# A priority above the mixers' early jobs for every weight piece of a hybrid decoder layer

## The chip, the cores and the metric

The kernel runs on one core of one Trainium2 chip. The metric is the device time of one execution in microseconds (us). Where three runs are shown, the median stands with the lowest and the highest. The profile is that of one execution, taken by the hardware profiler; its engines are PE (TensorE matmuls, with PEld for the weight loads into the array), DVE (VectorE), ACT (ScalarE), POOL (GpSimd) and SP, whose queue (SPq) issues most of the DMAs.

## The reference

One layer on 1024 tokens of width 1024, batch 1, all in float32:

```python
x = x + 0.5 * swiglu(rms_norm(x, ffn1_norm), w_gate1, w_up1, w_down1)   # 1024 -> 2816 -> 1024
x = x + hybrid_mixer(rms_norm(x, mix_norm), w_in, ..., w_out)
x = x + 0.5 * swiglu(rms_norm(x, ffn2_norm), w_gate2, w_up2, w_down2)
return rms_norm(x, final_norm)
```

The mixer projects the normed input once (`w_in`) and gives half of the columns to an HGRN2 recurrence (4 heads of 128, evaluated in chunks of 64 tokens) and half to an RWKV-7 recurrence (8 heads of 64, whose state is updated token by token in the reference). The outputs of both go through `w_out`.

## The kernel before

**Tiling.** Activations are kept with the features on the 128 partitions and 512 tokens along the free axis, so the sequence is two blocks, b=0 and b=1. A weight matrix is read in pieces of 128 x 512 float32 (256 KB). Each product is done as three matmuls in a rounded float32 format: a value is split into a rounded part `hi` and the remainder `lo`, and hi x hi, hi x lo and lo x hi are summed (`mm3`, lines 99 to 101).

**A piece of weights.** `load_piece` makes one: a DMA on SP's queue into `w_raw` (L76), the rounding to `w_hi` on ACT and the subtraction that gives `w_lo` on DVE (`split`, L67 and L68). `w_raw` has 7 buffers in the first and the last stage and 5 in the middle one; `w_hi` and `w_lo` have 3 each, for the whole program. A piece of four 128 x 128 weight tiles feeds 12 matmuls. The units of the feed-forward stages, which combine gate and up for both blocks with fewer products, load and split their pieces by functions of their own (`unit`, `load_raw`, `split_w`, L250 and the same L67 and L68).

**Stages.** Stage 1 is the first feed-forward part for most of the work of both blocks (`ffn_both`). Stage 2 holds, for each block, the input projection (`project_in`, whose low-rank part is L590), the mixers and, for b=1, its first feed-forward part (`ffn`); then the output projection and second feed-forward part of b=0. Stage 3 is the output projection of b=1 and the second feed-forward part (`ffn_both` again).

**The mixers.** For RWKV the work goes by two groups of head pairs: `rwkv_pair` (L752 to L821: shifts, decays, the gram matrices at L810), `rwkv_solve` (31 steps of two dependent DVE operations each, L842 and L843, and small matmuls at L865 and L873), `rwkv_chain` (chunk after chunk through PE, ACT and DVE: L890 to L908) and `rwkv_post` (normalisation, gating). `hgrn_head` does a head of the other recurrence (L665 to L744).

**What sets the order.** The engines' instruction streams are fixed before the run by a scheduler that simulates the program: among the instructions that are ready, an engine takes the one with the smallest priority number. That number is the place of the instruction in the program; `tc.high_priority(n)` lowers it by n for what is inside. On the chip each stream is then run in that order, with semaphores. A tile can be written only when one of its buffers is free. The numbers that are used:

- none: most matmuls, and all of `hgrn_head`;
- `AHEAD` = 6000: the weight pieces, the gains and splits of the activations (`gain_split`, L168 to L172), the sums of squares (L137, L139), the gates, and what empties PSUM (L614 in `project_in`, L235 and L455 after the down projections);
- `AHEAD - LATER`: the operands of the units (`Versions`);
- `SOON` = 20000: the RWKV jobs, from `rwkv_pair` to `rwkv_post`, called the mixers' early jobs here. 20000 is more than the count of instructions in front of any of them, so they come before everything else.

Of the kernel before, what the change touches and what calls it, by code (L numbers as in the profile page):

```python
# [36 lines left out]
AHEAD = 6000  # L37
RMS_AT = 4
UP_AT = 3
SOON = 20000  # L40

COLS = {}
_n = 0
# [21 lines left out]
def split(E, raw, hi, lo):  # L65
    nc = E.nc
    nc.scalar.copy(out=hi, in_=raw)  # L67
    nc.vector.tensor_tensor(out=lo, in0=raw, in1=f32(hi), op=ALU.subtract)  # L68
    return Half(hi, lo)


def load_piece(E, src):
    m = src.shape[1]
    with E.tc.high_priority(AHEAD):
        raw = E.wraw.tile([P, 512], F32, name="w_raw")
        E.nc.sync.dma_start(out=raw[:, :m], in_=src)  # L76
        hi = E.whl.tile([P, 512], F32R, name="w_hi")
        lo = E.whl.tile([P, 512], F32R, name="w_lo")
        return split(E, raw[:, :m], hi[:, :m], lo[:, :m])


def load_w(E, src, n):

    out = []
    for i in range(0, n, 4):
        m = min(4, n - i) * P
        w = load_piece(E, src[:, i * P:i * P + m])
        out += [w[:, c:c + P] for c in range(0, m, P)]
    return out
# [475 lines left out]
def project_in(E, b, xs, g, win, wtok, midway, early):  # L565
# [15 lines left out]
    for i, (at, m, dst) in enumerate(((NG, NLOW, lraw), (0, NG, sgl))):  # L581
        p = E.psf.tile([P, TB], F32, name="psf")[0:m]
        for k in range(KD):
            if k % 3 == 0:
                w = load_piece(E, wtok[:, k * NL:min(k + 3, KD) * NL])
            c = k % 3 * NL + at
            if i == 0 and k == 1:
                rms()
            for n, (u, x) in enumerate(((w.hi, h[k].hi), (w.hi, h[k].lo), (w.lo, h[k].hi))):
                nc.tensor.matmul(p, u[:, c:c + m], x, start=k + n == 0, stop=k == KD - 1 and n == 2)  # L590
        with tc.high_priority(AHEAD):
            e = E.ev.tile([P, TB + 1], F32, name="ev")
            nc.vector.tensor_tensor(out=e[0:m, 1:], in0=p, in1=r[0:m], op=ALU.mult)
            nc.gpsimd.tensor_copy(out=e[0:m, 0:1], in_=E.carry[0:m, b, 12 + i:13 + i])
            if b + 1 < NB:
                nc.gpsimd.tensor_copy(out=E.carry[0:m, b + 1, 12 + i:13 + i], in_=e[0:m, TB:TB + 1])
            shift(E, dst, e[0:m], 12 + i)
# [31 lines left out]
    for two in ((0, 1), (2, 3)):  # L629
        ps = [E.psf.tile([P, TB], F32, name="psf") for _ in two]  # L630
        for k in range(KD):
            w = load_piece(E, wtok[:, KD * NL + k * TB:KD * NL + (k + 1) * TB])
            for t, p in zip(two, ps):
                x = h[k][:, t * P:(t + 1) * P]
                nc.tensor.matmul(p, x.hi, w.hi, start=k == 0, stop=False)  # L635
                nc.tensor.matmul(p, x.lo, w.hi, start=False, stop=False)  # L636
                nc.tensor.matmul(p, x.hi, w.lo, start=False, stop=k == KD - 1)
        with tc.high_priority(AHEAD):
            for t, p in zip(two, ps):
                e = E.ft.tile([P, TB], F32, name="ft")  # L640
                nc.scalar.activation(out=e, in_=p, func=AF.Copy, scale=rt[:, t:t + 1])
                nc.sync.dma_start(out=pd["i"][t * P:(t + 1) * P], in_=e)
# [291 lines left out]
def mixer_pairs(E, b, gi, pd, low):  # L934

    pairs = []
    g = SimpleNamespace()
    for jj in range(2):
        p = rwkv_pair(E, b, 2 * gi + jj, jj, pd, low, g)
        pairs.append(p)  # L940
    next(pairs[0])
    yield
    g.ra = E.rw.tile([P, 2, NC, 2, C], F32, name="ra")
    g.bkt = E.rw.tile([P, NC, 2, P], F32, name="bkt")
    g.uv = E.rw.tile([P, NC, 2, P], F32, name="uv")
    g.wc = E.rw.tile([P, 2, NC], F32, name="wc")
    g.bonus = [E.dram.tile([P, TB], F32, name=f"bonus{jj}") for jj in range(2)]
    g.y = g.ra.rearrange("p j c x s -> p j (c x s)")[:, :, 0:TB]
    E.nc.gpsimd.memset(g.uv[C:P], 0.0)
    next(pairs[0], None)  # L950
    for _ in pairs[1]:
        pass
    yield g


def mixer(E, b, g, low, sgl, pd, od):
    second = mixer_pairs(E, b, 1, pd, low)
    for gi in range(2):
        with E.tc.high_priority(SOON):
            if gi:  # L960
# [130 lines left out]
def tile_hybrid_macaron(ctx: ExitStack, tc: tile.TileContext, x, cols, wgu1, wd1, win, wtok, w2a2, g2, wout, wgu2, wd2, nf_row, out, out_last):  # L1091
# [55 lines left out]
    with stage(hp=8, ap=4, wraw=5, ft=4, ev=2, rw=1, rm=4, t4=2, sh=6, sr=9, po=3, mc=1):  # L1147
# [3 lines left out]
        for b in range(NB):  # L1151
# [21 lines left out]
            def early(pd, low):  # L1173
                if b == 0:
                    mixer_constants(E, w2a2, g2)
                with tc.high_priority(SOON):
                    gs.extend(g for g in mixer_pairs(E, b, 0, pd, low) if g)
# [108 lines left out]
```

## Time and profile before

| | |
|---|---|
| median of 3 runs | 2110.25 us (2108.37 to 2115.01) |
| the profiled execution | 2111.05 us, its span 2109.0 us |
| PE | 2041.3 us busy, 97% of the span, 10840 matmuls |
| DVE | 1458.7 us, 69% |
| ACT | 980.4 us, 46% |
| weight pieces | 632 rounded on ACT and split on DVE, pieces of the units among them |
| loads of weights from `load_piece` and the units | 528 direct 256 KB loads, median 2.7 to 3.1 us from issue to landing |

Stage 1 lasts to about 570 us, stage 2 to about 1486 us and stage 3 to the end. A busy PE is not PE at its peak: its clock is granted by a throttle, and the profile gives the granted share for any stretch. Idle time of DVE or ACT costs nothing as long as PE has work; idle time of PE is the time that can be won.

### The profile page before, as it was taken

How to read it: one execution, taken by the hardware profiler on the slowest of the kernel's cores; microseconds unless marked ns; L12 is line 12 of the kernel's file. 1: busy time of each engine (PE TensorE's matmuls, PEld its weight loads, DVE VectorE, ACT ScalarE, POOL GpSimd, SP SyncE). 2: the span in 40 equal slices, each digit the busy share in tenths (PEclk: the TensorE clock that was granted, in tenths of full speed). 3: DMA queues.
4: the chain of work that ended last, by engine and by line, in shares of the span. 5: the costliest groups of instructions: out<-in, count | busy, mean ns of one | idle time of the engine just before them, and what ended most of it. 6: DMA issues, size and time to landing. Idle time of an engine off the chain costs nothing.

```text
span 2109.0 us, 29209 instructions
## 1 busy us (share of the span) xinstructions
PE 2041.3 (97%) x10840; PEld 1632.1 (77%) x10840; DVE 1458.7 (69%) x2455; ACT 980.4 (46%) x1595; POOL 36.5 (2%) x68
## 2 busy tenths in 40 slices
PE   8999999999999998998999999999999999999998
PEld 6778888888777766876777767877788788888887
DVE  7886455465876848877877679968676764554665
ACT  6443323234656646555557456546443433332353
POOL 0000000000110000000000000000000000000000
PEclk9999999999999999999999999999999999999999
DMA  6322212122644444444444554334433212121132
GB/s 195 87 79 55 66 41 70 33 57 72 200 146 145 135 132 140 126 111 126 147 144 134 158 168 125 108 83 144 149 98 118 79 55 65 40 71 35 56 110 80
DMA packets 146926, 220.39 MB, mean 104 GB/s; under 512 B 34752, under 2 KB 46528, under 8 KB 146784
## 3 DMA queue, kind: packets, MB, share of 16 engines
q1 hardware_dynamic: 145920, 217.18, 34.1%
q8 instruction: 85, 1.39, 0.3%
q10 hardware_dynamic: 864, 1.36, 0.2%
q14 instruction: 57, 0.47, 0.1%
HBM read 182.30 MB, written 36.18 MB: 104 GB/s over the span
## 4 chain that ended last, share of the span: by engine, by line
PE 86%; DVE 8%; issue 2%; ACT 2%; DMA 2%; SPq 0%; ACTq 0%; DVEq 0%
PE psf L101 19%; PE psf L100 19%; PE psf L99 19%; PE hq L101 3%; PE hq L100 3%; PE hq L99 3%; PE rq L99 2%; PE rq L100 2%; PE rq L101 2%; DVE w_lo L68 2%; PE rq L810 1%; PE psf L635 1%; PE rq L899 1%; PE psf L590 1%; PE psf L636 1%
## 5 line engine op out<-in xcount | busy, mean ns | idle before, releaser
L67 ACT CAST w_hi<-w_raw 128x512 fp32r<-128x512 f32 (+2 forms) x632 | 387.3, 614 | 832.4 <-PE psf L100 485.7
L68 DVE TENSOR_TENSOR w_lo<-w_raw,w_hi 128x512 fp32r<-128x512 f32 (+2 forms) x632 | 424.0, 675 | 158.3 <-ACT w_hi L67 156.8
L99 PE MATMUL psf<-v,w_hi 128*128 128x512 f32 x1072 | 419.5, 391 | 7.1 <-ACT v L67 4.0
L100 PE MATMUL psf<-v,w_hi 128*128 128x512 f32 x1072 | 418.8, 391 | 0.2 <-DVE v L68 0.2
L101 PE MATMUL psf<-v,w_lo 128*128 128x512 f32 x1072 | 418.6, 390 | 0.0
L101 PE MATMUL psf<-h_hi,w_lo 128*128 128x512 f32 x704 | 280.1, 401 | 10.3 <-DVE w_lo L68 10.3
L100 PE MATMUL psf<-h_lo,w_hi 128*128 128x512 f32 x704 | 281.9, 401 | 5.2 <-DVE h_lo L68 5.2
L99 PE MATMUL psf<-h_hi,w_hi 128*128 128x512 f32 x704 | 280.3, 399 | 4.1 <-ACT h_hi L67 3.3
L99 PEld LDWEIGHTS psf<-v,w_hi 128*128 128x128 f32 x1072 | 202.0, 188 | 53.0 <-ACT v L67 5.9
L100 PEld LDWEIGHTS psf<-v,w_hi 128*128 128x128 f32 x1072 | 202.1, 188 | 43.1 <-DVE v L68 1.3
L101 PEld LDWEIGHTS psf<-v,w_lo 128*128 128x128 f32 x1072 | 202.0, 188 | 42.0
L101 PEld LDWEIGHTS psf<-h_hi,w_lo 128*128 128x128 f32 x704 | 134.1, 190 | 42.0 <-DVE w_lo L68 14.0
L100 PEld LDWEIGHTS psf<-h_lo,w_hi 128*128 128x128 f32 x704 | 134.1, 190 | 36.0 <-DVE h_lo L68 7.7
L99 PEld LDWEIGHTS psf<-h_hi,w_hi 128*128 128x128 f32 x704 | 133.9, 190 | 34.5 <-ACT h_hi L67 4.6
L315 DVE TENSOR_TENSOR ft<-psf,ft 128x512 f32<-128x512 f32 x84 | 58.0, 691 | 111.1 <-PE psf L101 109.1
L101 PE MATMUL hq<-a,w_lo 128*128 128x512 f32 x288 | 112.3, 390 | 1.7 <-DVE w_lo L68 1.7
L99 PE MATMUL hq<-a,w_hi 128*128 128x512 f32 x288 | 112.3, 390 | 1.0 <-ACT w_hi L67 1.0
L100 PE MATMUL hq<-a,w_hi 128*128 128x512 f32 x288 | 112.1, 389 | 0.0
L101 PEld LDWEIGHTS hq<-a,w_lo 128*128 128x128 f32 x288 | 54.1, 188 | 13.7 <-DVE w_lo L68 2.6
L99 PEld LDWEIGHTS hq<-a,w_hi 128*128 128x128 f32 x288 | 54.1, 188 | 12.9 <-ACT w_hi L67 1.8
L100 PEld LDWEIGHTS hq<-a,w_hi 128*128 128x128 f32 x288 | 54.1, 188 | 11.2
L99 PE MATMUL rq<-a,w_hi 128*128 128x512 f32 x160 | 62.2, 389 | 0.0
(377 smaller groups left out, 3108.2 us busy)
## 6 DMA issues: line engine op xcount, KB each, us to landing
w_raw<-in_wgu_dram SPq DMA_DIRECT2D x240, 256.0 KB, 3.0
w_raw<-in_wd_dram SPq DMA_DIRECT2D x128, 256.0 KB, 2.7
w_raw<-in_win_dram SPq DMA_DIRECT2D x96, 256.0 KB, 3.0
w_raw<-in_wtok_dram SPq DMA_DIRECT2D x32, 256.0 KB, 3.0
w_raw<-in_wout_dram SPq DMA_DIRECT2D x32, 256.0 KB, 3.1
park<-xp SPq DMA_DIRECT2D x16, 256.0 KB, 3.1
ft<-od SPq DMA_DIRECT2D x16, 256.0 KB, 3.3
xp<-in_x_dram SPq DMA_DIRECT2D x15, 256.0 KB, 3.7
```

Of the source, the lines that this page charges most:

```text
L67: nc.scalar.copy(out=hi, in_=raw)
L68: nc.vector.tensor_tensor(out=lo, in0=raw, in1=f32(hi), op=ALU.subtract)
L99: E.nc.tensor.matmul(ps, w.hi, x.hi, start=start and i == 0, stop=False, **on)
L100: E.nc.tensor.matmul(ps, w.hi, x.lo, start=False, stop=False, **on)
L101: E.nc.tensor.matmul(ps, w.lo, x.hi, start=False, stop=(i == n - 1), **on)
L315: self.E.nc.vector.tensor_tensor(out=t, in0=p, in1=t, op=ALU.add)
L590: nc.tensor.matmul(p, u[:, c:c + m], x, start=k + n == 0, stop=k == KD - 1 and n == 2)
L635: nc.tensor.matmul(p, x.hi, w.hi, start=k == 0, stop=False)
L636: nc.tensor.matmul(p, x.lo, w.hi, start=False, stop=False)
L810: PE.matmul(gps[hh][:, c, :], bk[r, c0 + c, :, :], g.ra[r, jj, c0 + c, :, :], start=True, stop=True)
L899: PE.matmul(u[C:P, jj, :], E.theta[:, jj, cc, :], E.zbd[:, jj, :, :], start=True, stop=True, tile_position=(0, C))
```

## The change

The loading, rounding and splitting of a piece in `load_piece` gets a priority offset of 40000 in place of 6000. No instruction is added or removed; what may change is the place of instructions in the streams of SP, ACT and DVE, and through it that of others. The pieces of the units (`unit`) keep 6000.

```diff
 SOON = 20000
+FIRST = 40000
...
 def load_piece(E, src):
     m = src.shape[1]
-    with E.tc.high_priority(AHEAD):
+    with E.tc.high_priority(FIRST):
         raw = E.wraw.tile([P, 512], F32, name="w_raw")
         E.nc.sync.dma_start(out=raw[:, :m], in_=src)
         hi = E.whl.tile([P, 512], F32R, name="w_hi")
         lo = E.whl.tile([P, 512], F32R, name="w_lo")
         return split(E, raw[:, :m], hi[:, :m], lo[:, :m])
```

## The prediction

> **What bounds the kernel now.** I read the page first: the span, the engines, the chain that ended last, the groups of the weight pieces.
>
> ```profile
> span 2109.0 us, 29209 instructions
> PE 2041.3 (97%) x10840; PEld 1632.1 (77%) x10840; DVE 1458.7 (69%) x2455; ACT 980.4 (46%) x1595; POOL 36.5 (2%) x68
> ...
> L67 ACT CAST w_hi<-w_raw 128x512 fp32r<-128x512 f32 (+2 forms) x632 | 387.3, 614 | 832.4 <-PE psf L100 485.7
> L68 DVE TENSOR_TENSOR w_lo<-w_raw,w_hi 128x512 fp32r<-128x512 f32 (+2 forms) x632 | 424.0, 675 | 158.3 <-ACT w_hi L67 156.8
> ```
>
> PE is the bound, and 2109.0 - 2041.3 = 67.7 us of the span are all that any reordering can take out of PE's idle time; DVE and ACT have room. ACT's roundings mostly wait for PE to give a buffer back (485.7 us of idle time by that row), so the pieces are as far ahead as three buffers allow, and a higher priority can't bring them further ahead: it can only serve them sooner once a buffer is free.
>
> Then the busy time by stage, which says where PE idles, and PE's waits inside stage 2 and in the first 100 us (total, number, longest).
>
> ```profile
> 0.00:570.00 570.00, 556.35 (x2431) 456.49 (x2432) 367.99 (x575) 232.59 (x392) 3.17 (x11) 1.00 0.30 86
> 570.00:1486.00 916.00, 877.80 (x5758) 678.82 (x5756) 709.55 (x1292) 514.17 (x801) 33.38 (x58) 0.98 0.45 135
> ```
>
> ```profile
> PE psf L101 <- DVE w_lo L68: 11.2, 8, 4.4
> PE psf L590 <- DVE w_lo L68: 5.3, 2, 4.2
> PE psf L100 <- DVE h_lo L68: 5.2, 4, 4.1
> PE psf L99 <- ACT h_hi L67: 3.3, 3, 1.9
> PE rq L114 <- DVE po L68: 3.0, 4, 1.6
> ```
>
> ```profile
> PE hq L101 <- DVE w_lo L68: 1.7, 2, 0.9
> ...
> PE hq L99 <- ACT w_hi L67: 1.0, 2, 0.5
> PE psf L99 <- ACT w_hi L67: 0.5, 1, 0.5
> ```
>
> Of the 38.2 us that PE idles in stage 2 (916 - 877.8), 11.2 + 5.3 = 16.5 us are waits for the small part of a weight piece. With 1.7 + 1.0 + 0.5 us in stage 1, weights cost 19.7 us of idle PE in the whole program. That is the direct prize.
>
> Idle PE has a second price: the granted clock. Three stretches of half clock follow such waits (the column after POOL is the clock).
>
> ```profile
> 694.20:697.60 3.40, 3.40 (x8) 2.69 (x9) 3.40 (x9) 3.22 (x4) 0.00 (x0) 0.50 0.62 190
> 1001.40:1011.60 10.20, 8.20 (x19) 4.54 (x20) 9.73 (x18) 1.67 (x3) 0.00 (x0) 0.50 0.52 154
> 1151.60:1155.00 3.40, 3.40 (x9) 2.64 (x9) 3.29 (x12) 0.66 (x2) 0.00 (x0) 0.50 0.83 245
> ```
>
> Half of each stretch is lost: 1.7 + 5.1 + 1.7 = 8.5 us. The ceiling of the change is therefore 19.7 + 8.5 = 28.2 us.
>
> **What a wait for weights looks like.** The timeline of DVE over the longest one, and the matmuls of PE that end this wait and that at 692 us.
>
> ```profile
> 1142.95 3.33 DVE L779 RECIPROCAL sr<-sr 128x512 f32<-128x512 f32 x1
> ...
> 1147.29 1.21 DVE L787 TENSOR_TENSOR_SCAN sr<-scanm,sr 128x512 f32<-128x512 f32 x1
> ...
> 1150.13 0.68 DVE L68 TENSOR_TENSOR w_lo<-w_raw,w_hi 128x512 fp32r<-128x512 f32 x1
> ```
>
> ```profile
> 1142.65 1.12 ACT L67 CAST w_hi<-w_raw 128x512 fp32r<-128x512 f32 x2
> ```
>
> ```profile
> 1150.86 0.50 PE L101 MATMUL psf<-h_hi,w_lo 128*128 128x512 f32 x1 [4.42 <-DVE w_lo L68]
> ```
>
> ```profile
> 694.12 0.75 PE L101 MATMUL psf<-h_hi,w_lo 128*128 128x512 f32 x1 [1.70 <-DVE w_lo L68]
> ```
>
> Both pieces were rounded by 1143.8, but DVE took a reciprocal of a mixer job, then the solve's steps and other mixer jobs, and split the first piece at 1150.13. With the change the split stands ahead of all those that had not begun when the rounding ended; only the reciprocal, begun at 1142.95, can still be in front.
>
> **The change part by part, in numbers.** Loads, roundings and splits cost what they cost now; the sum is made of PE's idle time.
>
> *Six waits at L101 outside the solves*: 11.2 - 4.42 - 1.70 = 5.1 us. The splits there wait behind mixer jobs and evictions while three of them queue up. The mixer jobs that go back by one to three splits (0.68 us each) are covered by PE's own projection matmuls. I take 5.1; bounds 2.5 (half come back) and 5.1.
>
> *The two waits inside the solves* (694 and 1150 us): 4.42 + 1.70 + 1.7 + 1.7 = 9.5 us. Here what is late next is the solve, a chain of DVE steps that has no slack of its own; it goes back by the splits put in front, and the reciprocal's 3.33 us stay in the stream. PE's order is fixed, so it stands at the solve's matmuls if they come late. I take half, 4.8; bounds 0 and 9.5.
>
> *The start of the second projection* (L590): 5.3 + 5.1 = 10.4 us at most. The stream there:
>
> ```profile
> 998.41 3.35 DVE L121 RECIPROCAL po<-po 128x512 f32<-128x512 f32 x1
> 1001.67 0.60 DVE L68 TENSOR_TENSOR w_lo<-w_raw,w_hi 128x480 fp32r<-128x480 f32 x1
> 1002.18 0.68 DVE L923 TENSOR_TENSOR po<-ra,po 128x512 f32<-128x512 f32 x1
> 1002.78 0.75 DVE L172 SCALAR_TENSOR_TENSOR h_lo<-xp,vec,h_hi 128x512 fp32r<-128x512 f32 x1
> ```
>
> Behind the same reciprocal and one more mixer job comes the small part of the next activation, which keeps its priority and which the next matmuls need. With the weights ready PE stops there, about 1 us later than it was released here. I take 3; bounds 0 and 10.4.
>
> *The waits of stage 1*: 3.2 us, caused by sums of squares and gates with an older place at the same priority. I take 2.6; bounds 0 and 3.2.
>
> Together -15.5 us. On the other side:
>
> *The start.* SP's queue, PE's first matmul, and what the DMAs moved in forty slices of 1.5 us from 0 to 60:
>
> ```profile
> 0.82 0.38 SPq L76 DMA_DIRECT2D w_raw<-in_wgu_dram  x1
> 1.25 1.37 SPq L1116 DMA_DIRECT2D xp<-in_x_dram  x3
> 2.66 9.23 SPq L76 DMA_DIRECT2D w_raw<-in_wgu_dram  x9
> ```
>
> ```profile
> 7.42 0.80 PE L99 MATMUL hq<-v,w_hi 128*128 128x512 f32 x1 [7.42 <-ACT v L421]
> ```
>
> ```profile
> GB/s 0 90 311 351 397 330 205 335 314 285 306 242 303 246 311 391 184 279 315 253 5 0 183 143 34 0 164 139 203 18 175 51 130 79 96 12 163 0 20 154
> ```
>
> The three tiles of x had the offset 6000 and an older place, so they stood behind one weight load; now up to six more loads of 256 KB have buffers and go first. Issues alone cost 6 x 0.46 = 2.7 us (1.37 us for three); the bytes, 1.57 MB at the 351 to 397 GB/s of the fullest slices, 4.0 to 4.5. x0 goes by ACT's queue, so PE still begins, and then waits for the next tiles. I take +3; bounds 0 and +6.
>
> *Work of priority 6000 that now stands behind splits*: the activations' parts at the stage changes (5.2 + 3.3 us of waits above, 7 of them). One split each is 7 x 0.68 = 4.8 us; I take +2, as the three buffers are mostly full there; bounds 0 and +4.8.
>
> *The chains.* PE's array loads that waited for the chain's hops in stage 2:
>
> ```profile
> PEld rq L892 <- DVE mst L908: 6.9, 23, 0.4
> PEld rq L903 <- ACT uv L900: 6.8, 17, 0.7
> PEld rq L899 <- DVE zbd L894: 6.7, 18, 0.5
> ```
>
> 58 waits, none of which has a weight operation in front of it by priority now. DVE spends about a fifth of its time on splits (424.0 of 2109.0 us), so some 12 hops would meet one, a third of a us each on average: +4 if PE covers none. I take +3, adding nothing else for the mixers; bounds 0 and 58 x 0.65 = +38.
>
> Sum: -15.5 + 3 + 2 + 3 = -7.5 us on the profiled execution's 2111.05 us, so 2103.5; that execution is 0.8 us over the median of the runs shown, so 2102.7, rounded to 2103.
>
> What the Trainium skill says of the clock, in "TensorE: Matmul & The Clock Gate", section "HAM oscillation — how this bites in real kernels", is that gaps over about 3.4 us throttle the array. By that rule the 1.70 us wait would have cost no clock, and the term of the solves would be 9.5 - 1.7 = 7.8 at most. The trace disagrees: half clock stands in the row at 694.20 right behind that wait. I keep the row.
>
> **The rivals.**
>
> *The stall moves on* (net within 6 us). Every wait of PE for weights lets DVE catch up. Take it away, and PE arrives earlier at the next mixer matmul, whose operands come from the same DVE stream with the same 3.3 us reciprocals. For it: both long waits lie right behind a reciprocal, and PE's row at L114 (3.0 us, for `po`) shows such a wait already. Against it: six of the eight waits at L101 share 5.1 us, and what they push back, 0.68 us a split, is small beside the projection's matmuls that PE has at hand. The terms of the solves and of the second projection are then 0 and the rest is -5.1 - 2.6 + 8 = about 0: 2110.
>
> *All of it is won.* PE's own projections cover what the mixers lose, and the stretch at 1001 us keeps its clock: -28.2 with the start's +3 and half of the other costs, about -22: 2089. Against it stands the activation's part at 1002.78.
>
> *Slower: the chain pays.* The 32 chunk steps (2 blocks, 2 groups, 8 chunks) hop from PE to ACT or DVE and back three times each. If a rounding or split stands ahead of every second hop that PE waits for now, that is 29 x 0.65 = 19 us, and the sum is -15.5 + 5 + 19 = +8.5: 2119. It decides from (15.5 - 5) / 0.65 = 16 hops on. For it: these jobs were first in every queue and are now second. Against it: a piece comes only every 12 matmuls, when a buffer is given back, and PE gives none back while it stands at a hop.
>
> *The change does nothing there.* Pieces can't pass a full set of three buffers, and a queue in order can't overtake what runs; if the splits that PE waits for are free to run only when the mixer job in front has begun, the waits of stage 2 stay. Then -2.6 stands against the start's +3: within 3 us of now. It is counted with the first rival.
>
> **How the numbers follow.** What a measurement of this kernel can tell from no change is about 0.3%, 6.3 us: faster means below 2103.9, slower above 2116.6. The forecast has 0.42, its own range 2095 to 2109, two thirds of it faster than that bound when the start is cheap; the moved stall 0.28; all won 0.12; slower 0.18, a part of which stays within the bound. Faster: 0.27 + 0.12 + 0.06 = 0.45. Slower: 0.16. The rest, 0.39, is the same. The range takes in most of "all won" and the lower part of the chain's price: 2088 to 2118.
>
> **What would show it.** In the changed kernel PE's waits for `w_lo` and `w_hi` should fall from 19.7 to under 5 us in all, with no half clock behind 692 and 1146 us; on DVE, a split should follow its rounding with no mixer job between. The start should show SP issuing seven weight loads ahead of x, and PE's first 100 matmuls some 3 us later. If the stall has moved, the rows for L114, L865, L873, L899 and L590 with `h_lo` grow by what the weights' rows lose. If the chain pays, the three array-load rows above grow by 10 us or more. A time above 2117 or waits for weights still over 10 us make the prediction wrong.

## The result, and the profile after

The changed kernel takes 2135.9 us, the median of 4 runs (2131.7 to 2139.5), against 2110.3 us for the kernel before on the same chip: a ratio of 1.0119 (95% interval 1.0105 to 1.0133), 25.6 us slower. 2103 had been forecast, with a range of 2088 to 2118. The profiled execution took 2139.49 us, 28.4 more than the profiled one before, so its rows show 3 us more of the loss than the medians do.

The page of the changed kernel: span, engines and the two groups of the weight pieces. All lines of the code stand one further down than before.

```profile
span 2137.8 us, 29162 instructions
PE 2048.7 (96%) x10840; PEld 1647.8 (77%) x10840; DVE 1464.8 (69%) x2455; ACT 974.2 (46%) x1591; POOL 37.9 (2%) x68
...
L68 ACT CAST w_hi<-w_raw 128x512 fp32r<-128x512 f32 (+2 forms) x632 | 387.5, 613 | 820.2 <-PE psf L101 455.3
L69 DVE TENSOR_TENSOR w_lo<-w_raw,w_hi 128x512 fp32r<-128x512 f32 (+2 forms) x632 | 424.5, 674 | 176.6 <-ACT w_hi L68 170.5
```

The work is the same: the same 632 roundings and splits with the same durations. PE's idle part of the span grew from 67.7 to 89.1 us (2137.8 - 2048.7); the other 7.4 us of the longer span are PE's busy time, 2048.7 against 2041.3, at a granted clock of 0.97 over the whole execution where it was 0.99.

PE's waits in the changed kernel (total, number, longest), cut to the groups that the prediction spoke of.

```profile
PE hq L100 <- ACT v L68: 13.2, 1, 13.2
PE rq L115 <- DVE po L69: 12.4, 4, 8.5
PE hq L100 <- ACT v L422: 12.0, 2, 8.0
PE psf L100 <- ACT h_hi L68: 11.2, 3, 7.6
PE rq L874 <- ACT sr L68: 5.1, 1, 5.1
...
PE hq L100 <- ACT w_hi L68: 1.0, 2, 0.5
```

The waits for weights, 19.7 us before, are down to the last row: 1.0 us. The change does what it says, and PE stands longer all the same, for `v`, `po`, `h_hi` and `sr`.

Where that is, the busy time by stage shows.

```profile
0.00:570.00 570.00, 554.88 (x2419) 454.75 (x2420) 366.99 (x573) 231.98 (x390) 2.94 (x10) 1.00 0.30 85
570.00:1510.00 940.00, 888.21 (x5771) 695.09 (x5769) 712.82 (x1289) 506.49 (x797) 34.95 (x58) 0.95 0.42 127
```

Taken from the first matmul of one stage to the first of the next, stage 1 takes 572.1 us (569.3 before), stage 2 948.8 (917.5) and stage 3 to its last matmul 610.4 (615.8): +2.8, +31.3 and -5.4. Up to the middle of stage 2 nothing is lost for long: PE's 6000th matmul begins 2.4 us earlier than before, near 1186 us. The 8400th, early in stage 3, begins 30.7 us later. Part of that builds up in between: from 1183.90 to 1491.40 PE is busy for 289.52 of 307.50 us at a granted clock of 0.94, where from 1186.15 to 1485.80 it was busy for 291.33 of 299.65 us at 0.99. Most of it is at the very end of stage 2. PE there, in the kernel before and in the changed one:

```profile
1486.79 0.73 PE L99 MATMUL hq<-v,w_hi 128*128 128x512 f32 x2 [1.00 <-ACT v L67]
...
1495.15 0.50 PE L99 MATMUL hq<-v,w_hi 128*128 128x512 f32 x1 [3.44 <-ACT v L67]
```

```profile
1491.06 0.40 PE L906 MATMUL ry<-gram,uv 128*64 128x64 f32 x8
1494.28 0.77 PE L115 MATMUL rq<-po,bones_r 128*128 128x512 f32 x1 [2.81 <-DVE po L69]
...
1505.29 0.79 PE L115 MATMUL rq<-po,bones_r 128*128 128x512 f32 x1 [8.54 <-DVE po L69]
...
1520.95 0.80 PE L100 MATMUL hq<-v,w_hi 128*128 128x512 f32 x1 [13.16 <-ACT v L68]
```

Before, PE went from the last down projection straight into stage 3 and only waited 3.44 us for the last HGRN head. Now the last RWKV chain (L906) and its two posts (L115) run when PE has nothing else left: 2.81 + 8.54 + 13.16 = 24.5 us of waiting, in a stretch at half clock:

```profile
1493.30:1527.40 34.10, 11.42 (x25) 7.74 (x26) 20.02 (x23) 9.86 (x17) 0.00 (x0) 0.50 0.59 197
```

SP's queue tells how late the RWKV mixer is. `po<-bonus` is the load in its last post. Before:

```profile
1445.57 0.33 SPq L926 DMA_DIRECT2D po<-bonus  x1
...
1489.61 0.32 SPq L744 DMA_DIRECT2D od<-sh  x1
```

and after:

```profile
1506.11 0.32 SPq L927 DMA_DIRECT2D po<-bonus  x1
...
1515.41 7.21 SPq L980 DMA_DIRECT2D ft<-od  x8
```

So the RWKV mixer ends 60.5 us later. From that load to the first matmul of stage 3 it takes 1520.95 - 1506.11 = 14.8 us. Before, 1445.57 + 14.8 = 1460.4 lay 26.4 us ahead of 1486.79: by this estimate the mixer had 26.4 us to spare. The other 60.5 - 26.4 = 34.1 us are what the first matmul of stage 3 is later (1520.95 - 1486.79). The two agree by the way the estimate is made, and so are no check of it; that other kernels keep nearly the same distance of 14.8 us, shown below, is one.

**Where the mixer loses time.** One solve, in the queue of SP: the store of its result (`thd`), and the reloads of it (`theta`, eight DMAs, and two of `t1d`), on which its last matmuls and the chain wait. Before:

```profile
728.81 0.48 SPq L847 DMA_DIRECT2D thd<-t  x1
...
731.77 0.85 SPq L858 DMA_DIRECT2D theta<-thd  x2
732.73 0.92 SPq L852 DMA_DIRECT2D sr<-t1d  x2
733.71 1.96 SPq L858 DMA_DIRECT2D theta<-thd  x4
735.71 0.45 SPq L758 DMA_DIRECT2D sr<-pd_r  x1
736.20 0.92 SPq L858 DMA_DIRECT2D theta<-thd  x2
```

After, the same solve:

```profile
742.19 0.48 SPq L848 DMA_DIRECT2D thd<-t  x1
743.96 0.93 SPq L77 DMA_DIRECT2D w_raw<-in_wtok_dram  x2
744.93 0.42 SPq L849 DMA_DIRECT2D t1d<-t  x1
745.53 3.05 SPq L77 DMA_DIRECT2D w_raw<-in_wtok_dram  x3
...
756.27 0.43 SPq L859 DMA_DIRECT2D theta<-thd  x1
757.26 1.68 SPq L77 DMA_DIRECT2D w_raw<-in_wgu_dram  x2
...
764.63 1.42 SPq L859 DMA_DIRECT2D theta<-thd  x3
```

Between the store and the last reload stand weight loads, and SP's queue runs in order, so what a weight load waits for, the reloads wait for too. SP's waits in that stretch of the changed kernel:

```profile
SPq L77 <- DVE w_lo L69: 10.7, 13, 1.3
```

Thirteen times a weight load waited there until a split gave its raw buffer back. From the store to the issue of the last reload the four solves took 7.9, 9.0, 7.9 and 7.3 us before and take 23.4, 11.5, 8.5 and 13.3 now: 32.1 against 56.7, +24.6 us.

The other part of a solve is its DVE steps. The four stretches from the reload of `lam` to the store of `thd`, summed (length, then busy PE, PEld, DVE), before and after:

```profile
sum 203.70, PE 194.36 PEld 156.96 DVE 191.26 ACT 121.13 POOL 0.20; mean PE 48.59 PEld 39.24 DVE 47.82 ACT 30.28 POOL 0.05
```

```profile
sum 225.71, PE 218.01 PEld 178.41 DVE 207.38 ACT 130.94 POOL 0.31; mean PE 54.50 PEld 44.60 DVE 51.84 ACT 32.73 POOL 0.08
```

DVE is busy for 94% and 92% of these stretches: there is no room for a split that doesn't make the solve longer. The operations of the split line alone take 50.74 us of them before and 61.68 after; the stretches are 22.0 us longer, so the split line accounts for about half of that.

These sums over four solves, 24.6 and 22.0 us, must not be set against the 60.5 us, because the two blocks don't simply follow each other. The first solve of block 0 stores its `lam` 10.2 us late, and the last `po<-bonus` of block 0 comes 63.2 us late (1060.39 against 997.22). But the first `lam` store of block 1 is only 21.5 us late (1142.14 against 1120.60): the time between the blocks has covered 41.7 us. Block 1 then adds 39.0 us. Its two solves give 15.4 of these (reloads 21.8 against 15.2, stretches 109.5 against 100.7), and 18.0 come between the last `po<-bonus` of its first group and the `lam` store of the second (74.6 us, where it was 56.6). What is left, 5.6 us, is the balance of the other parts. What the solves are worth in time, the experiments have to tell.

### The profile page after: what moved, and what is told of

It is laid out like the page before. It is cut to its first block, busy times and chain, and to the rows that moved or that the text cites. A ratio compares the mean times of both kernels' runs of the same rounds, so it can differ in the third digit from the quotient of the medians.

```text
span 2137.8 us, 29162 instructions
## 1 busy us (share of the span) xinstructions
PE 2048.7 (96%) x10840; PEld 1647.8 (77%) x10840; DVE 1464.8 (69%) x2455; ACT 974.2 (46%) x1591; POOL 37.9 (2%) x68
## 4 chain that ended last, share of the span: by engine, by line
PE 48%; DVE 3%; DMA 1%; ACT 1%; issue 1%; SPq 0%; DVEq 0%; ACTq 0%
PE psf L100 10%; PE psf L101 10%; PE psf L102 10%; PE hq L100 2%; PE hq L101 2%; PE hq L102 2%; PE rq L102 1%; PE rq L101 1%; PE rq L100 1%; PE rq L811 1%; PE rq L900 1%; DVE w_lo L69 1%; PE rq L893 0%; PE rq L904 0%; DMA ft<-od 0%
## 5 line engine op out<-in xcount | busy, mean ns | idle before, releaser
L100 PE MATMUL psf<-v,w_hi 128*128 128x512 f32 x1072 | 419.4, 391 | 6.0 <-ACT v L68 4.2
L100 PE MATMUL psf<-h_hi,w_hi 128*128 128x512 f32 x704 | 283.4, 404 | 12.8 <-ACT h_hi L68 11.2
L100 PEld LDWEIGHTS psf<-v,w_hi 128*128 128x128 f32 x1072 | 202.1, 189 | 50.5 <-ACT v L68 5.8
L100 PEld LDWEIGHTS psf<-h_hi,w_hi 128*128 128x128 f32 x704 | 134.8, 192 | 43.6 <-ACT h_hi L68 12.2
L100 PE MATMUL hq<-a,w_hi 128*128 128x512 f32 x288 | 112.3, 390 | 1.0 <-ACT w_hi L68 1.0
L100 PEld LDWEIGHTS hq<-a,w_hi 128*128 128x128 f32 x288 | 54.1, 188 | 12.9 <-ACT w_hi L68 1.9
L101 PEld LDWEIGHTS hq<-a,w_hi 128*128 128x128 f32 x288 | 54.1, 188 | 11.9 <-DVE a L69 0.7
L100 PE MATMUL rq<-a,w_hi 128*128 128x512 f32 x160 | 62.2, 389 | 0.0
```

The source lines that it names most:

```text
L100: E.nc.tensor.matmul(ps, w.hi, x.hi, start=start and i == 0, stop=False, **on)
L101: E.nc.tensor.matmul(ps, w.hi, x.lo, start=False, stop=False, **on)
```

## The experiments

All were run in rounds beside the kernel before, whose median was 2108.7 to 2110.1 us in the five batches. Times are medians, ratios are against the kernel before. "Alone" and "ahead" stand for an offset of 40000 in place of 6000.

### The three steps of a piece apart

`load_piece` gets an offset for each of its steps; -1 and -2 keep the places that the steps had among themselves.

```diff
-    with E.tc.high_priority(FIRST):
-        raw = ...
-        E.nc.sync.dma_start(out=raw[:, :m], in_=src)
-        hi = ...
-        lo = ...
-        return split(E, raw[:, :m], hi[:, :m], lo[:, :m])
+    load, rnd, sub = E.at
+    with E.tc.high_priority(load):
+        raw = ...
+        E.nc.sync.dma_start(out=raw[:, :m], in_=src)
+    hi = ...
+    lo = ...
+    with E.tc.high_priority(rnd - 1):
+        E.nc.scalar.copy(out=hi, in_=raw[:, :m])
+    with E.tc.high_priority(sub - 2):
+        E.nc.vector.tensor_tensor(out=lo, in0=raw[:, :m], in1=f32(hi), op=ALU.subtract)
```

In this form the buffers of `hi` and `lo` are asked for outside any offset. No run has the form with three equal offsets, so what it does to the order by itself is not shown.

Load ahead alone, `E.at = (FIRST, AHEAD, AHEAD)`:

> Only the DMA of a piece has the offset 40000; rounding and split keep 6000. Theory A (the mixers' early jobs form one serial chain; roundings on ACT and splits on DVE in front of its steps lengthen it until PE has no other work at the end of stage 2): the chain isn't touched, so 2110 + 3 for the later x at the start = 2111 to 2115. Theory B (SP's queue: weight loads in front of the mixers' loads and stores hold the chain up): most of the loss is here, 2128 to 2138.

Rounding ahead alone, `(AHEAD, FIRST, AHEAD)`:

> Only the rounding on ACT has 40000. Theory A: the chain's ACT steps go back by 0.61 us each where a rounding is in front, DVE's don't; a part of the loss, 2112 to 2122. Theory B: no loss, 2107 to 2112.

Split ahead alone, `(AHEAD, AHEAD, FIRST)`:

> Only the split on DVE has 40000. Theory A: most of the chain's steps are DVE's (62 in a solve), so the larger part of the loss, 2118 to 2132, while PE's waits for w_lo in stage 2 fall from 16.5 us to under 4. Theory B: only the gain of those waits, 2098 to 2108.

In the same batch the changed kernel with the mixers put back on top, so that the pieces stand above all other work but below the mixers' early jobs:

```diff
-SOON = 20000
+SOON = 60000
```

> Pieces keep 40000, and the mixers' early jobs get 60000, so pieces stand only above the work of priority 6000 (evictions, gates, activation parts). Theory A: the loss is gone but for the start, 2109 to 2115. Theory C (the loss comes from evictions, gates and activation parts that stand behind the pieces): still 2128 to 2138.

Then the pairs, `(FIRST, FIRST, AHEAD)`, `(FIRST, AHEAD, FIRST)` and `(AHEAD, FIRST, FIRST)`:

> The load and the rounding of each piece at 40000, the split at the old 6000. Alone the load gave -2.4 us and the rounding +17.5. Theory 1 (the rounding on ACT is what delays the mixers' chains of jobs, and an earlier load lets it come still earlier): 2130 to 2140, the last post of the RWKV mixer at 1490 us or later (before 1455, after 1514). Theory 2 (the parts act each by itself): the sum, about 2125, last post near 1465. Theory 3 (only the whole step ahead does the harm): within 10 us of the kernel before.

> The load and the split at 40000, the rounding at the old 6000. Theory 1 (the rounding on ACT does the harm, and nothing but the split brings a gain): 2085 to 2095, as with the split alone (2089.6). Theory 2 (the parts add): 2087. Theory 3 (the harm comes when loads are early and pieces are finished early, whatever engine does it): 2105 or more.

> The rounding and the split at 40000, the load at the old 6000. Theory 1 (the rounding delays the mixers, the split only saves waits of PE for w_lo): 2115 to 2130, no waits for w_lo over 3 us in total, and the RWKV mixer's last post at 1480 us or later. Theory 2 (the parts add): +17.5 - 20 = about 2107. Theory 3 (the load is needed for the harm): 2085 to 2095.

| ahead | us | ratio (95%) | `thd` store to last reload, four solves | last `po<-bonus` | last HGRN output |
|---|---|---|---|---|---|
| nothing | 2109.7 | 1 | 32.1 us | 1445.6 | 1489.6 |
| load | 2107.3 | 0.9987 (0.9977 to 0.9997) | 88.0 | 1473.5 | 1460.6 |
| rounding | 2127.1 | 1.0083 (1.0068 to 1.0098) | 31.1 | 1455.3 | 1506.4 |
| split | 2089.6 | 0.9908 (0.9893 to 0.9923) | 33.6 | 1462.5 | 1442.7 |
| load, rounding | 2105.2 | 0.9978 (0.9968 to 0.9987) | 78.2 | 1470.0 | 1457.7 |
| load, split | 2122.4 | 1.0059 (1.0044 to 1.0074) | 63.9 | 1492.1 | 1444.1 |
| rounding, split | 2087.7 | 0.9902 (0.9887 to 0.9916) | 34.0 | 1460.8 | 1438.6 |
| all three | 2135.9 | 1.0119 (1.0105 to 1.0133) | 56.7 | 1506.1 | 1483.2 |
| all three, mixers on top | 2101.3 | 0.9963 (0.9948 to 0.9977) | 32.1 | 1448.7 | 1482.6 |

My first theory after the result, that the loss is the splits' delay of the mixers, fell at once: alone they win 20 us, though the last `po<-bonus` comes 17 us later there. The next, that the rounding does it, stood on the second row and fell with the rows "load, rounding" and "rounding, split". What the rows do show: the four solves' reloads are late in all four kernels of this table in which the load stands above the mixers (56.7 to 88.0 us), and in no other (31.1 to 34.0). SP in the kernel with the load alone ahead, same solve as above:

```profile
737.41 0.48 SPq L853 DMA_DIRECT2D thd<-t  x1
...
764.68 0.42 SPq L864 DMA_DIRECT2D theta<-thd  x1
```

27.3 us from store to last reload. That kernel still isn't slower: its RWKV mixer is 27.9 us late, about what it had to spare, and PE enters stage 3 at 1492.7, 19.2 us behind the last `po<-bonus`, after a wait of only 1.0 us. With the split ahead as well the spare time is gone: "load, split" and "all three", at 1492.1 and 1506.1, are 14.0 us apart there and 13.5 us in time.

So in most kernels the slower of two mixers holds stage 3 up. In the nine kernels of this study whose first matmul of stage 3 stands 14.0 to 14.8 us behind the last `po<-bonus`, RWKV is last. In five (the kernel before, the rounding alone, and the three with the mixers on top and a rounding ahead) the HGRN heads are: the 24th matmul of stage 3 ends 7.7 to 8.8 us behind their last output. In the other six (the load alone, the split alone, rounding and split, the split with the mixers on top, and later the solves on top with and without the chains) neither fits: the first matmul stands 6.7 to 23.3 us behind the last `po<-bonus`, with the HGRN heads long done. The row of the rounding alone follows its HGRN heads, 16.8 us later output and 17.5 us more time. SP and PE of that kernel:

```profile
1506.37 0.32 SPq L750 DMA_DIRECT2D od<-sh  x1
```

```profile
1511.72 0.80 PE L105 MATMUL hq<-v,w_hi 128*128 128x512 f32 x1 [8.95 <-ACT v L68]
```

### Split ahead with the mixers on top

`E.at = (AHEAD, AHEAD, FIRST)` and `SOON = 60000`:

> Load and rounding at 6000, split at 40000, the mixers' early jobs at 60000 above all of them. If the gain of the split alone (2089.6) comes from its standing above the units' evictions and gates at 6000, not above the mixers, this keeps it: 2080 to 2092, with the RWKV mixer's last post before 1465. If the gain comes from holding the mixers back, it falls away: 2100 to 2112.

2087.8 us, ratio 0.9896 (0.9882 to 0.9911). The gain of the split ahead is all there with the mixers on top, so it comes from passing other work (what stands at 6000, or has no offset), not from holding the mixers back.

### Only the DMAs put back

The changed kernel, with the solve's DMA issues (three for `lam`, and twelve from the store of `thd` to the last reload) in a `high_priority` of their own:

```diff
+        with E.tc.high_priority(FIRST):
             nc.sync.dma_start(out=lamd[...], in_=G[...])
...
+    with E.tc.high_priority(FIRST):
         nc.sync.dma_start(out=thd..., in_=th)
...
+                with E.tc.high_priority(FIRST):
                     nc.sync.dma_start(out=E.theta[...], in_=thd[...])
```

> The changed kernel, with the twelve-odd DMA issues of each solve (lam, th and their reloads) at 60000, above the pieces' 40000. Theory Q (SP's queue: weight loads, now first, hold back the solve's reloads; from the store of thd to the issue of the last theta reload the four solves took 56.7 us in all against 32.1 before, and 88.0 with the load alone ahead): this falls back to 30 to 36 us, the RWKV mixer's last post to 1475 to 1490 us (from 1514), the time to 2095 to 2112. Theory H (DVE's and ACT's queues: splits and roundings ahead of the chain's and the solve's hops do it, the reloads are only late with them): 2128 to 2140.

With the other DMAs of the RWKV mixer (L759, L804, L927, L932) and the HGRN output (L745) treated in the same way:

> As the former, and with the other DMAs of the RWKV mixer (the pairs' loads of r, k and v, the bonus out and back, the output) at 60000 too, with the HGRN heads' output store at 40000. Theory Q: as the former or up to 10 us better, 2090 to 2108, last post 1465 to 1485. Theory H: 2128 to 2140.

The solve's DMAs on top of "load, split":

> Load and split at 40000 and the rounding at 6000 (2122.4 us without the next), with the solves' DMAs at 60000. Theory Q: the load ahead costs only by SP's queue, so this comes to the split alone (2089.6): 2085 to 2100. Theory H: 2115 to 2125.

And with the first four tiles of x above the pieces too:

```diff
-        xs = load_x(0, prio=[AHEAD] * 4 + [AHEAD - 200] * 4)
+        xs = load_x(0, prio=[FIRST + AHEAD] * 4 + [AHEAD - 200] * 4)
```

> The mixers' DMAs above the pieces, and the first four tiles of x as well (offset 46000). Against the run without the x tiles: PE's gap at 11.3 us (4.0 us) gone and the time 2 to 4 us lower under any theory; Theory Q 2087 to 2105, Theory H 2125 to 2137.

Measured: 2122.3 us (ratio 1.0051, 1.0036 to 1.0066), 2125.0 (1.0065, 1.0048 to 1.0082), 2110.5 (1.0000, 0.9990 to 1.0010) and 2118.3 (1.0035, 1.0022 to 1.0047). The reloads are back to 33.3 us in the first of them, and the last `po<-bonus` comes at 1486.4 in place of 1506.1. So SP's queue is real: the solve's issues on top give back 13.6 of the 25.6 us, and 11.9 in "load, split". It isn't all: the first result lies between what both theories expected, and the mixer's other DMAs add nothing to it. The DVE part of the four solves is as long as in the changed kernel, 228.8 us. Putting x first brought stage 1 back from 572.0 to 568.3 us; the whole gained 6.7 us, more than the 2 to 4 expected, but this kernel's runs spread over 10 us.

### Which mixer jobs

The changed kernel with single jobs lifted above the pieces:

```diff
+TOP = 40000
...
-            rwkv_solve(E)
-            E.M[gi] = rwkv_chain(E, E.M[gi], g)
+            with E.tc.high_priority(TOP):
+                rwkv_solve(E)
+                E.M[gi] = rwkv_chain(E, E.M[gi], g)
```

> The changed kernel, with the whole of the solves and the chains (their DMAs too) at 60000, above the pieces; pairs and posts stay at 20000. With the solves' DMAs alone above it was 2122.3, with all mixer jobs above 2101.3. If the splits in front of the solve's DVE steps are the rest of the loss (the four solves' DVE part took 205 us before, 226 after): DVE part back to 203 to 210 us, last post's load at 1455 to 1475, 2100 to 2110. If the pairs are (57 and 57 us from a post to the next solve before, 68 and 75 after): 2115 to 2125.

The same around the pairs and the posts instead:

> The changed kernel, with the pairs and the posts at 60000; solves and chains stay at 20000, below the pieces. If the solves lose the most (SP's queue 24.6 us, DVE part 21 us): 2118 to 2130. If the pairs do: 2100 to 2112.

Around `rwkv_solve` alone, and around `rwkv_chain` alone:

> The changed kernel with the solves alone (DVE steps, copies and DMAs) at 60000, above the pieces; chains at 20000. The solves' DMAs alone gave 2122.3, solves and chains 2091.2. If the solves are the main loss: 2093 to 2105. If the chain's hops share it evenly: 2106 to 2118.

> The changed kernel with the chains alone at 60000; solves at 20000, below the pieces. If the chain's hops are what the change pays (the prediction's rival, 19 us, bounds 0 to 38): 2098 to 2117. If the solves are: 2125 to 2137.

| above the pieces | us | ratio (95%) | back of the changed kernel's 2135.9 |
|---|---|---|---|
| solves | 2098.1 | 0.9939 (0.9923 to 0.9956) | 37.8 |
| chains | 2132.5 | 1.0107 (1.0092 to 1.0122) | 3.4 |
| solves and chains | 2091.2 | 0.9921 (0.9899 to 0.9943) | 44.7 |
| pairs and posts | 2121.2 | 1.0058 (1.0040 to 1.0076) | 14.7 |
| all jobs | 2101.3 | 0.9963 (0.9948 to 0.9977) | 34.6 |

The largest part is the solves': alone on top they give back more than the whole loss. The rows don't add up (37.8 + 3.4 + 14.7 = 55.9, against 34.6 for all jobs), so they are no shares of the loss. The pairs and posts are worth 14.7 us alone. The chains' 3.4 is not clear of noise: the interval overlaps that of the changed kernel (1.0105 to 1.0133). The kernel with the solves on top has the reloads in one run again, with one weight load among them, where the changed kernel has fourteen in its first solve:

```profile
738.49 0.48 SPq L849 DMA_DIRECT2D thd<-t  x1
...
740.69 0.34 SPq L78 DMA_DIRECT2D w_raw<-in_wtok_dram  x1
741.41 0.82 SPq L860 DMA_DIRECT2D theta<-thd  x2
...
743.30 2.94 SPq L860 DMA_DIRECT2D theta<-thd  x6
```

Its four DVE stretches, summed:

```profile
sum 210.62, PE 208.46 PEld 170.44 DVE 195.21 ACT 125.59 POOL 0.33; mean PE 52.12 PEld 42.61 DVE 48.80 ACT 31.40 POOL 0.08
```

Reloads 32.1 and stretches 210.6 us are 24.7 and 15.1 us less than in the changed kernel. The first `lam` store of block 1 comes 26.0 us earlier than there (1116.11), and the last `po<-bonus` 39.2 us earlier (1466.95), beside 37.8 us of time. How much of this the DVE steps bring without the DMAs was not run: 37.8 - 13.6 = 24.2 us is only a difference. With the chains alone on top the reloads stay late (76 us over the four solves) and so does the last post, 1499.9.

Lifting all jobs gives back less than the solves and chains do, since then the HGRN heads, which have no priority of their own, are what ends last: 1482.6 against 1441.8.

### The rounding once more

`E.at = (AHEAD, FIRST, AHEAD)` and `(AHEAD, FIRST, FIRST)`, both with `SOON = 60000`:

> Load and split at 6000, rounding at 40000, the mixers' early jobs at 60000. If rounding alone costs its 17.5 us by passing the mixers' steps on ACT: 2105 to 2113. If by passing the units' own work of 6000 on ACT (activations' parts, gates, evictions): 2120 to 2130.

> Load at 6000, rounding and split at 40000, the mixers' early jobs at 60000. Rounding and split ahead gave 2087.7, the split alone with the mixers on top 2087.8. If what is gained comes from PE not waiting for pieces and the mixers then have slack: 2082 to 2090. If the rounding ahead costs once the mixers are on top: 2095 or more.

2113.0 us (1.0020, 1.0010 to 1.0029) and 2102.3 us (0.9967, 0.9955 to 0.9979). Of the 17.5 us that the rounding alone costs, 13 are gone once the mixers stand above it. But the second, expected at 2082 to 2090, is 14.6 us slower than without the mixers on top. In both the HGRN heads end last, at 1496.5 and 1482.0, and the times follow them. Why a rounding ahead makes these heads late, when no split is ahead below the mixers, isn't shown by these runs; it stays open.

Nothing here beats rounding and split ahead (2087.7) or the split ahead with the mixers on top (2087.8): 1.0% faster than the kernel before, and 2.3% faster than the changed one.

## Why the prediction was wrong

**The direct prize: right.** Waits for weights were to fall from 19.7 to under 5 us; they fell to 1.0. Half clock behind 692 and 1146 us is gone too, though it stands in other places now. At L591, the start of the second projection, PE waits 1.1 us for `h_lo` where it waited 5.3 for `w_lo`, so more of that term was won than the 3 us taken. The kernels with the split ahead and the load not come near the time of the rival "all of it is won" (2087.7 to 2089.6 for 2089; its own terms add up to 2087.6), but by other terms: with rounding and split ahead PE idles 57.1 us in place of 67.7, though its waits for weights fell by 18.0, and is busy for 2028.7 us in place of 2041.3. Where the shorter busy time comes from isn't shown. The ceiling itself was a little high: half of the stretch at 1001.40 was counted as 5.1 us, but PE was busy for 8.20 us of it, which makes 4.1.

**The start: right.** +3 forecast; PE's 100th matmul begins 3.8 us later (38.3 against 34.5), and 2.8 us are left at the end of stage 1, whose waits for weights are shorter. It is this wait of PE behind SP's first issues (ten weight loads, where seven had been forecast), and it went away when x was put first:

```profile
15.31 0.79 PE L100 MATMUL hq<-v,w_hi 128*128 128x512 f32 x1 [4.01 <-ACT v L422]
```

```profile
0.82 8.05 SPq L77 DMA_DIRECT2D w_raw<-in_wgu_dram  x10
8.92 3.65 SPq L1117 DMA_DIRECT2D xp<-in_x_dram  x7
```

**Work of 6000 behind splits: the number near, by luck.** PE's waits for the activations' parts were 5.2 + 3.3 = 8.5 us at L99 and L100; the row for `h_hi` above has 11.2 now, and for `h_lo` none is left there: +2.7 where +2 had been put. But 7.63 us of the 11.2 are one wait at 1205.79, where the output projection of b=0 begins, and it ends on no split. ACT's rounding waited there for a load of a mixer's output (`od`):

```profile
1205.12 0.62 ACT L68 CAST h_hi<-ft 128x512 fp32r<-128x512 f32 x1 [5.82 <-DMA ft<-od]
```

**The chains: small, as taken, and so their rival fell.** +3 was taken; lifting the chains above the pieces gave back 3.4 us, or 6.9 (44.7 - 37.8) with the solves lifted too, neither near the rival's 19. The three array-load rows, which were to grow by 10 us if the chain paid, shrank from 20.4 to 13.5:

```profile
PEld rq L904 <- ACT uv L901: 7.0, 19, 0.4
...
PEld rq L900 <- DVE zbd L895: 3.5, 10, 0.4
PEld rq L893 <- DVE mst L909: 3.0, 11, 0.4
```

The slower rival named the right sign, but another place than the one that paid.

**The step that failed: the two waits inside the solves.** The prediction gave this term a gain of 4.8 us with bounds 0 and 9.5. It said that the solve "has no slack of its own" and "goes back by the splits put in front", and set no price for that beyond losing the gain; in the chains' term it wrote "adding nothing else for the mixers". The runs give the price: with the solves alone above the pieces 37.8 us come back, more than the whole loss. Three things are missing in its working.

First, the bound looked only at the two moments where PE had waited for weights. But the priority works through all of the four solves, 203.7 us in which DVE was already 94% busy. They grew by 22.0 us.

Second, SP. The loads were counted as they pass the tiles of x at the start, and nowhere else. In stage 2 they pass the solve's own way through memory, fifteen issues a solve. The reloads take 24.6 us more over the four solves, and 13.6 us come back in time when these issues alone are put on top.

Third, the reason given against a slower outcome, that a piece comes only when PE gives a buffer back, holds where PE stands at a chain's hop. During a solve PE is busy with the projection (53.35 of the 53.35 us of the first, by the trace after) and gives buffers back all the time.

**What wasn't looked at: the end of stage 2.** The sum was made of PE's waits alone, as if a mixer that is later were covered by PE's other work. It is, for about 26.4 us. Most of that figure stood in the trace before: 41.2 us between the last `po<-bonus` at 1445.57 and PE's entry into stage 3 at 1486.79; the 14.8 us to take off come from the changed kernel. Beyond them the delay goes on into stage 3 (the nine kernels above), and the tail, at half clock, is where the 24.5 us of PE's three long waits are.

**The rival "the stall moves on"** was right in kind: PE's waits for `sr` at L874 (5.1 us) and `po` at L115 (12.4) are in the list that it named. It had them equal to what the weights' rows lose. They, `v` and `h_hi` have 41.9 us together, where the same four rows had 10.7 before: 31.2 us more, against 18.7 taken away.

## What to carry to other kernels

Before work is moved ahead of a chain of dependent jobs, write down how much later that chain may end before the next stage waits for it (here about 26 us), and count the moved work on every engine and queue over the whole length of the chain, not only where PE is seen waiting; a load on a shared in-order queue counts with what it waits for itself. Price the steps of a bundle one by one: here the split ahead wins 20 us, the load ahead costs nothing alone, and both together lose 13. Where one job of a chain is full on its engine, keep that job on top and let the moved work pass the others.

## What the runs showed of the hardware

A queue of DMA issues hands on the waits of whatever stands first. Thirteen waits for a raw buffer, 10.7 us in all and none longer than 1.3, and the issues of the fourteen weight loads themselves turned 7.4 us of reload issues into 22.4 (the first solve, from the store of `thd` to the start of the row with its last reloads).

The granted clock can fall after a short wait, and the length of the wait does not decide it alone. In the changed kernel PE had stood for 1.76 us before this matmul, and the stretch behind it ran at half clock (the column after POOL):

```profile
919.32 0.66 PE L690 MATMUL hq<-sh 128*64 128x32 f32 x16 [1.76 <-DVE sh L685]
```

```profile
919.90:926.70 6.80, 6.80 (x40) 5.10 (x37) 4.34 (x15) 1.60 (x3) 0.00 (x0) 0.50 0.15 41
```

The Trainium skill, in "TensorE: Matmul & The Clock Gate", section "HAM oscillation — how this bites in real kernels", gives about 3.4 us as the idle gap to stay under. This trace doesn't agree: 1.76 us was followed by 6.8 us at half clock.

Nor is a wait of such a length always followed by half clock. The prediction priced 1.7 us of clock for the wait of 1.70 us at 694.12 in the kernel before. With the rounding alone ahead the same matmul waited as long, and the clock stayed full behind it:

```profile
694.30 0.50 PE L107 MATMUL psf<-h_hi,w_lo 128*128 128x512 f32 x1 [1.70 <-DVE w_lo L84]
```

```profile
694.30:697.70 3.40, 3.40 (x15) 2.83 (x16) 3.40 (x9) 3.36 (x5) 0.00 (x0) 1.00 0.63 175
```

What else decides is not shown by these runs.

At the end of stage 2 of the changed kernel the clock came back only at 1527.40, 6.4 us after PE had begun to work again at 1520.95.
